# Shift and scale of a streaming-encoder layer: raw fp32 weights over four column groups in place of split weights over 8 columns

## Chip, cores and metric

The kernel runs on one NeuronCore of one Trainium2 chip. The metric is the device time in microseconds; each kernel is timed in several runs, and the median counts. A profile is one execution recorded by the hardware profiler. PE is the matmul engine (PEld its weight loads), DVE the vector engine, ACT the scalar engine, POOL the general one, SP the engine that issues most DMAs.

## The reference, cut to what matters

One layer works on 256 prompt rows and 32 sample rows of 2048 features. Each group has its own conditioning vector `c`; from it come shift, scale and gate, and the first two make `h`, which everything after multiplies with its weights:

```python
mod = jax.nn.silu(c) @ ada_w + ada_b            # (2 vectors of 2048) @ (2048, 3 * 2048)
shift, scale, gate = jnp.split(mod, 3, axis=-1)
h = rms_norm(x, g_pre) * (1.0 + scale[:, None]) + shift[:, None]
proj = h @ w_in                                  # (288 rows of 2048) @ (2048, 20480)
```

After that come a gated convolution, a retention with eight heads, two branch products and an output product. All data is fp32. Only shift and scale, 2 x 2048 x 2048 weights of `ada_w`, are touched by the change.

## The kernel before, in words

Features lie on the 128 partitions: 2048 features are 16 feature tiles, and `h` is held transposed, 128 features by 288 rows for each tile. A product of fp32 data is made of three faster products of type fp32r: `split` (L114) writes a value as `hi` (a cast on ACT, L116) plus `lo` (a subtraction on DVE, L117), and `accumulate` (L146) adds hi x hi, hi x lo and lo x hi (L151, L152, L154). Weights come from memory in loads of 1 MB (`weights`, L127, issued on SP at L131) into `raw` buffers, four of them and a fifth during the first phase. `split_weights` (L134) cuts a load into two pieces of 128 x 1024 and splits each into a `whi` and a `wlo` buffer; there are six of each in the first phase. A `raw` buffer is free for the next load when both of its pieces are split.

The first phase, which the change is in, makes `h` in four groups of four feature tiles (`GROUPS`) and starts on it at once:

- `norm_x` and `turn_x` normalise `x` and turn it, three PE transposes for each of 16 tiles (L257), copied out by ACT and DVE in turn (L258).
- `modulation` (L261) makes scale and shift of one group, 512 features each. The conditioning vectors are the stationary operand (`cs`, silu of c in hi and lo, and zeros around them, so that a slice of 8 columns holds them at rows 4 to 7 for shift or 0 to 3 for scale), and the split weights move, 512 columns at a time, into 8 rows of one PSUM tile (L273). A group takes eight loads (called steps below), each with four feature tiles of K for scale or for shift: two pieces, four products of `whi` and four of `wlo`. Then the 8 rows are copied out (`modrow`, L278), turned by four PE transposes (L282), and the rows of the parts are summed (L284).
- `make_h` (L288) adds bias and factors (L300 to L302), then per feature tile writes `h` (ACT L311 for the prompt, DVE L308 for the sample) and splits it into `hh` and `hl`.
- `first_products` (L313) multiplies the group with four blocks of 512 columns of `w_in` (`FIRST`), one 1 MB load and 48 matmuls each, and adds them into `firsts` (ACT L329 for the first group, DVE L331 for the rest).

The steps of the next group's modulation are put between the four blocks of the present group (the loop with `STEPS`): block 1, four steps, block 2, four steps, then blocks 3 and 4. The loads stand on SP in that same order. The tile framework then orders each engine's instructions by its own priorities, and every engine runs its list strictly in that order. After the first phase (from about 195 us on) PE runs the big products to the end.

Of the kernel before, what the change touches and what calls it, by code (L numbers as in the profile page):

```python
# [10 lines left out]
F32 = mybir.dt.float32  # L11
F32R = mybir.dt.float32r
AF = mybir.ActivationFunctionType
ALU = mybir.AluOpType
PSUM = bass.MemoryType.PSUM

P = 128
D = 2048
# [9 lines left out]
EPS = 1e-6  # L28
# [5 lines left out]
# in the first phase that many more  # L34
MORE_RAW, MORE_PARTS = 1, 2
PIECE = 1024
# feature tiles whose shift and scale come first, and so on
GROUPS = ((0, 4), (4, 8), (8, 12), (12, 16))
# the steps of each: two products of a part of K at a time, then h
STEPS = [sum(2 * min(4, b - k) + 1 for k in range(a, b, 4)) for a, b in GROUPS]  # L40
# rows of the vector table
R_SC, R_CW, R_CB, R_GP, R_AB = 0, 2, 5, 6, 7
NR = 8
# columns of w_in
# [7 lines left out]
# columns of w_in whose products start before all of h is there (2 WC each): q and k of four heads, v of some  # L52
# [3 lines left out]
# decay table: one head's columns  # L56
# [3 lines left out]
def tables():  # L60
    """Rotary and decay constants of the shapes."""
# [25 lines left out]
    # k's factor, in what multiplies it  # L87
# [6 lines left out]
def hybrid_step(ctx: ExitStack, tc, x_prompt, x_sample, c_prompt, c_sample, state_conv, state_ret,  # L94
# [19 lines left out]
    def split(src, hi, lo):  # L114
        """src as hi + lo exactly, each of 12 significant bits."""
        A.copy(out=hi, in_=src)  # L116
        V.tensor_tensor(out=lo, in0=src, in1=hi.bitcast(F32), op=ALU.subtract)  # L117
# [3 lines left out]
    def buffer(tag, size, dtype, bufs, extra):  # L121
        """One of bufs in turn, and of extra ones while there is room for them"""
# [4 lines left out]
    def weights(w, k0, n, col, width):  # L127
        """Rows of n feature tiles from k0, some columns."""
# [5 lines left out]
    def split_weights(raw):  # L134
        """(first row, hi, lo) of each piece"""
# [10 lines left out]
    def accumulate(ps, hi, lo, f, k0, xh, xl, first, last):  # L146
        """ps += (x @ w).T for one tile of w's columns, by the products of the parts"""
# [10 lines left out]
    def product(w, col, xh, xl):  # L158
        """Two tiles of (x @ w[:, col : col + WC]).T, accumulated in PSUM."""
# [22 lines left out]
    def rstd_of(ss, n, width):  # L182
        """(ss / n + EPS) ** -0.5"""
# [10 lines left out]
    cs = const.tile([P, NK, 12], F32R, name="cs")  # L194
# [7 lines left out]
    with tc.tile_pool(name="start", bufs=1, reuse_waits="tile") as st:  # L202
        more.append(st)
        A.preload_act_table(AF.Sigmoid)
        # vectors as rows of P features; they turn in one step
# [23 lines left out]
        V.memset(cs.bitcast(F32), 0.0)  # L229
        split(sc, cs[:, :, 4:6], cs[:, :, 6:8])  # L230
# [9 lines left out]
        def norm_x():  # L240
            """the norm before, then features on the partitions"""
# [19 lines left out]
        def modulation(ka, n):  # L261
            """scale and shift of n feature tiles, the parts' products on rows of their own"""
            pm = aux_tile()
            width = n * P
            step = KH * WC // width
            for part in range(2):
                rows_at = slice(4 - 4 * part, 12 - 4 * part)
                for k0 in range(0, NK, step):
                    for kb, hi, lo in split_weights(weights(ada_w[0], k0, step, (1 - part) * D + ka * P, width)):
                        for k in range(hi.shape[1]):  # L270
                            kt = k0 + kb + k
                            for w in (hi, lo):
                                nc.tensor.matmul(pm[:8, :width], cs[:, kt, rows_at], w[:, k, :],  # L273
                                                 start=(part == 0 and kt == 0 and w is hi),
                                                 stop=(part == 1 and kt == NK - 1 and w is lo))
                    yield
            ms = st.tile([8, 2 * WC], F32, name="modrow", tag="modrow", bufs=2)
            A.copy(out=ms[:, :width], in_=pm[:8, :width])  # L278
            yield
            po = aux_tile()  # L280
            for f in range(n):
                nc.tensor.transpose(out=po[:, 8 * f:8 * f + 8], in_=ms[:, f * P:(f + 1) * P], identity=ident[:8, :8])  # L282
            mod = st.tile([P, 4, 2, 2], F32, name="mod", tag="mod", bufs=2)
# [427 lines left out]
```

## Time and profile before

| what | value |
|---|---|
| time, median of 3 runs | 1395.62 us (1394.64 to 1400.27) |
| span of the profiled execution | 1394.6 us |
| mean granted PE clock | 0.996 |
| busy over the span: PE, DVE, ACT | 98%, 63%, 44% |
| first of the first products on PE | 47.44 us |
| first products of the four groups begin at | 47.4, 88.2, 129.0, 169.9 us |
| end of the first phase | about 195 us |

The profiled execution's own time is its span, 1394.6 us; the runs' median is 1.0 us above it. Matmul rows overlap, so the distance between two starts says what a matmul costs in a stream, not the length of a row. Rows with "x4" merge four instructions that follow on one another. In a row of a matmul, "128\*8 128x512" means a stationary operand of 128 rows by 8 columns, and a moving one of 128 x 512.

### The profile page before, as it was taken

Reading aid. Unit: us, or ns where it says so; the run is one execution under the profiler, and the core shown is the slowest. Engines: PE = TensorE matmul, PEld = TensorE weight load, DVE = VectorE, ACT = ScalarE, POOL = GpSimd, SP = SyncE. Lnnn points to the kernel's source line nnn. Section 1 sums busy time; section 2 is a strip of 40 time slices with the busy share of each in tenths; the row PEclk is TensorE's granted clock in tenths of the full one; section 3 lists DMA queues with packets and bytes.
Section 4 is the critical chain, followed back from the end, with each engine's and each line's share of the span. In section 5 each row is a group of like instructions: output and inputs, shape, how many; then the busy total and the mean of one; then the engine's idle time right before and its main releaser. Section 6 shows DMA issues by size and latency. Waiting matters only on the chain.

```text
span 1394.6 us, 23833 instructions
## 1 busy us (share of the span) xinstructions
PE 1362.2 (98%) x9978; PEld 1300.2 (93%) x9978; DVE 872.9 (63%) x1426; ACT 612.0 (44%) x885; POOL 9.4 (1%) x16
## 2 busy tenths in 40 slices
PE   4999999999999999999999999999999999999996
PEld 1677898999999999999999999999999999999995
DVE  5888977555545866666777868766555334555443
ACT  6876645544444333333333333333333333334442
POOL 0000000000000000000000000000000000000000
PEclk9999999999999999999999999999999999999998
DMA  9988853444444667566565657574544555556531
GB/s 330 333 305 309 302 173 126 156 152 139 160 160 142 190 210 215 185 207 207 188 206 192 215 183 223 178 247 153 179 154 162 172 160 173 160 173 227 160 104 68
DMA packets 234069, 267.79 MB, mean 192 GB/s; under 512 B 5077, under 2 KB 208133, under 8 KB 233349
## 3 DMA queue, kind: packets, MB, share of 16 engines
q1 hardware_dynamic: 227968, 256.22, 55.6%
q10 hardware_dynamic: 5992, 10.04, 2.5%
q8 instruction: 78, 1.28, 0.4%
q14 instruction: 31, 0.25, 0.0%
HBM read 261.75 MB, written 4.49 MB: 191 GB/s over the span
## 4 chain that ended last, share of the span: by engine, by line
issue 67%; PE 31%; DVE 1%; DMA 0%; ACT 0%; SPq 0%; POOL 0%; DVEq 0%; POOLq 0%; ACTq 0%
PE acc L151 8%; PE acc L152 7%; PE acc L154 7%; PE aux L273 4%; PE aux L390 1%; PE aux L392 1%; PE aux L257 1%; PE aux L391 1%; PE aux L490 0%; DMA x<-in_x_prompt_dram 0%; DVE wlo L117 0%; PE aux L404 0%; DVE x L680 0%; PE aux L440 0%; ACT xT L247 0%
## 5 line engine op out<-in xcount | busy, mean ns | idle before, releaser
L117 DVE TENSOR_TENSOR wlo<-raw,whi 128x1024 fp32r<-128x1024 f32 x448 | 542.0, 1221 | 402.8 <-ACT whi L116 402.3
L116 ACT CAST whi<-raw 128x1024 fp32r<-128x1024 f32 x448 | 464.1, 1049 | 583.4 <-PE acc L152 550.6
L152 PE MATMUL acc<-hl,whi 128*128 128x288 f32 x2304 | 632.4, 296 | 0.0
L151 PE MATMUL acc<-hh,whi 128*128 128x288 f32 x2304 | 631.1, 296 | 0.0
L151 PEld LDWEIGHTS acc<-hh,whi 128*128 128x128 f32 x2304 | 432.4, 188 | 3.2 <-issue 1.1
L152 PEld LDWEIGHTS acc<-hl,whi 128*128 128x128 f32 x2304 | 433.2, 188 | 1.0 <-DVE hl L117 0.3
L154 PE MATMUL acc<-hh,wlo 128*128 128x288 f32 x2304 | 406.2, 293 | 0.0
L154 PEld LDWEIGHTS acc<-hh,wlo 128*128 128x128 f32 x2304 | 341.5, 188 | 0.2 <-issue 0.2
L525 DVE SCALAR_TENSOR_TENSOR gbc<-raw,sc,gbc 128x256 f32<-128x256 f32 x240 | 100.4, 476 | 10.5 <-DMA raw<-in_ada_w_dram 10.5
L152 PE MATMUL acc<-ml,whi 128*128 128x288 f32 x256 | 70.9, 297 | 0.0
L151 PE MATMUL acc<-mh,whi 128*128 128x288 f32 x256 | 70.8, 299 | 0.0
L152 PE MATMUL acc<-yl,whi 128*128 128x288 f32 x256 | 70.0, 295 | 0.0
L151 PE MATMUL acc<-yh,whi 128*128 128x288 f32 x256 | 70.0, 296 | 0.0
L151 PE MATMUL acc<-ch,whi 128*128 128x288 f32 x256 | 70.0, 296 | 0.0
L152 PE MATMUL acc<-cl,whi 128*128 128x288 f32 x256 | 69.5, 294 | 0.0
L273 PE MATMUL aux<-wlo,cs 128*8 128x512 f32 x128 | 51.3, 401 | 0.4
L273 PE MATMUL aux<-whi,cs 128*8 128x512 f32 x128 | 51.6, 403 | 0.0
L151 PEld LDWEIGHTS acc<-mh,whi 128*128 128x128 f32 x256 | 48.3, 189 | 0.1
L152 PEld LDWEIGHTS acc<-cl,whi 128*128 128x128 f32 x256 | 48.3, 189 | 0.0
L152 PEld LDWEIGHTS acc<-yl,whi 128*128 128x128 f32 x256 | 48.2, 188 | 0.1
L152 PEld LDWEIGHTS acc<-ml,whi 128*128 128x128 f32 x256 | 48.1, 188 | 0.1
L151 PEld LDWEIGHTS acc<-yh,whi 128*128 128x128 f32 x256 | 48.1, 188 | 0.1
(188 smaller groups left out, 967.2 us busy)
## 6 DMA issues: line engine op xcount, KB each, us to landing
raw<-in_w_in_dram SPq DMA_DIRECT2D x144, 1024.0 KB, 5.2
raw<-in_ada_w_dram SPq DMA_DIRECT2D x48, 1024.0 KB, 6.2
raw<-in_w_branch_dram SPq DMA_DIRECT2D x32, 1024.0 KB, 5.7
raw<-in_w_out_dram SPq DMA_DIRECT2D x16, 1024.0 KB, 5.7
x<-in_x_prompt_dram SPq DMA_DIRECT2D x2, 1024.0 KB, 6.1
out_dram<-ns SPq DMA_DIRECT2D x16, 128.0 KB, 2.9
x<-in_x_prompt_dram ACTq DMA_DIRECT2D x1, 2048.0 KB, 8.0
out_dram<-x ACTq DMA_DIRECT2D x4, 512.0 KB, 2.8
```

The lines of the kernel that those rows point to most:

```text
L116: A.copy(out=hi, in_=src)
L117: V.tensor_tensor(out=lo, in0=src, in1=hi.bitcast(F32), op=ALU.subtract)
L151: nc.tensor.matmul(ps, hi[:, k, fs], xh[:, k0 + k, :], start=first and k == 0, stop=False)
L152: nc.tensor.matmul(ps, hi[:, k, fs], xl[:, k0 + k, :], start=False, stop=False)
L154: nc.tensor.matmul(ps, lo[:, k, fs], xh[:, k0 + k, :], start=False, stop=last and k == n - 1)
L257: nc.tensor.transpose(out=px[:, g * P:g * P + n], in_=x[:n, g, k * P:(k + 1) * P], identity=ident[:n, :n])
L273: nc.tensor.matmul(pm[:8, :width], cs[:, kt, rows_at], w[:, k, :], start=(part == 0 and kt == 0 and w is hi), stop=(part == 1 and kt == NK ...
L390: nc.tensor.matmul(ps, a[0][ai], b[0][bi], start=first, stop=False)
L391: nc.tensor.matmul(ps, a[0][ai], b[1][bi], start=False, stop=False)
L392: nc.tensor.matmul(ps, a[1][ai], b[0][bi], start=False, stop=last)
L525: V.scalar_tensor_tensor(out=ga[:, b], in0=raw[:, k], scalar=sc[:, kt, b:b + 1], in1=ga[:, b], op0=ALU.mult, op1=ALU.add)
```

## The change

`cs` becomes 32 columns of fp32, silu of both vectors in the first two and zeros behind, not split. A step loads two feature tiles of K for both shift and scale, in two DMAs of 512 KB into one `raw` buffer, and the raw fp32 weights are the moving operand: four products for each step, each with 32 stationary columns, at four positions of the array and of the PSUM tile's partitions (`tile_position`): 0 and 32 for an even feature tile's shift and scale, 64 and 96 for an odd one's. The `raw` buffer is free when the last of the four has run. The 128 rows are copied out, and four fp32 products with `pick` (a 128 x 4 matrix of ones and zeros) turn and sum them; the vector engine reads the result in place, without the sum of L284. Line numbers behind this place in the file are four or five higher after the change: L273 becomes L281, L278 L285, L282 L289, L300 to L302 L305 to L307, L311 L316.

```diff
-    cs = const.tile([P, NK, 12], F32R, name="cs")
+    cs = const.tile([P, NK, 32], F32, name="cs")
+    pick = const.tile([P, 4], F32, name="pick")
+    rows4 = ident.rearrange("p (k s r) -> p k s r", k=2, s=2)
+    V.tensor_tensor(out=pick.rearrange("p (s b) -> p s b", s=2), in0=rows4[:, 0, :, 0:2], in1=rows4[:, 1, :, 0:2], op=ALU.add)
...
-        V.memset(cs.bitcast(F32), 0.0)
-        split(sc, cs[:, :, 4:6], cs[:, :, 6:8])
+        V.memset(cs, 0.0)
+        V.tensor_copy(cs[:, :, 0:2], sc)
...
-            step = KH * WC // width
-            for part in range(2):
-                rows_at = slice(4 - 4 * part, 12 - 4 * part)
-                for k0 in range(0, NK, step):
-                    for kb, hi, lo in split_weights(weights(ada_w[0], k0, step, (1 - part) * D + ka * P, width)):
-                        for k in range(hi.shape[1]):
-                            kt = k0 + kb + k
-                            for w in (hi, lo):
-                                nc.tensor.matmul(pm[:8, :width], cs[:, kt, rows_at], w[:, k, :],
-                                                 start=(part == 0 and kt == 0 and w is hi),
-                                                 stop=(part == 1 and kt == NK - 1 and w is lo))
-                    yield
-            ms = st.tile([8, 2 * WC], F32, name="modrow", tag="modrow", bufs=2)
-            A.copy(out=ms[:, :width], in_=pm[:8, :width])
+            step = KH * WC // (2 * width)
+            for k0 in range(0, NK, step):
+                raw = buffer("raw", KH * WC, F32, RAW, MORE_RAW)
+                v = raw.rearrange("p (k s c) -> p k s c", k=step, s=2)
+                for s in range(2):
+                    c0 = s * D + ka * P
+                    nc.sync.dma_start(out=v[:, :, s, :], in_=ada_w[0, k0 * P:(k0 + step) * P, c0:c0 + width]
+                                      .rearrange("(k p) c -> p k c", p=P))
+                for k in range(step):
+                    kt = k0 + k
+                    for s in range(2):
+                        g = 32 * (2 * (kt % 2) + s)
+                        nc.tensor.matmul(pm[g:g + 32, :width], cs[:, kt, :], v[:, k, s, :], start=kt < 2, stop=kt >= NK - 2,
+                                         tile_position=(0, g))
+                yield
+            ms = st.tile([P, 2 * WC], F32, name="modrow", tag="modrow", bufs=2)
+            A.copy(out=ms[:, :width], in_=pm[:, :width])
             yield
             po = aux_tile()
             for f in range(n):
-                nc.tensor.transpose(out=po[:, 8 * f:8 * f + 8], in_=ms[:, f * P:(f + 1) * P], identity=ident[:8, :8])
-            mod = st.tile([P, 4, 2, 2], F32, name="mod", tag="mod", bufs=2)
-            V.tensor_reduce(out=mod[:, :n], in_=po[:, :8 * n].rearrange("p (f s r b) -> p f s b r", s=2, r=2, b=2),
-                            axis=mybir.AxisListType.X, op=ALU.add)
-            return mod[:, :n, 0, :], mod[:, :n, 1, :]
+                nc.tensor.matmul(po[:, 4 * f:4 * f + 4], ms[:, f * P:(f + 1) * P], pick, start=True, stop=True)
+            mod = po[:, :4 * n].rearrange("p (f s b) -> p f s b", s=2, b=2)
+            return mod[:, :, 1, :], mod[:, :, 0, :]
```

The change also moves instructions. On PE, the place behind block 2 of group 0's first products, where the second four steps of group 1's modulation end (before: `aux_460` is the modulation's PSUM tile, `whi_681` block 3's weights).

```order
L273 MATMUL aux_460<-whi_663,cs_87 8x512
L273 MATMUL aux_460<-wlo_664,cs_87 8x512
L273 MATMUL aux_460<-whi_663,cs_87 8x512
L273 MATMUL aux_460<-wlo_664,cs_87 8x512
L151 MATMUL acc_675<-hh_85,whi_681 128x288
```

The same place on PE after the change, where `aux_371` is that PSUM tile, `raw_466` to `raw_487` are the four steps and `whi_504` is block 3's weights:

```order
L154 MATMUL acc_407<-hh_85,wlo_439 128x288 x2
L281 MATMUL aux_371<-raw_466,cs_87 32x512 x4
L281 MATMUL aux_371<-raw_473,cs_87 32x512 x4
L281 MATMUL aux_371<-raw_480,cs_87 32x512 x4
L281 MATMUL aux_371<-raw_487,cs_87 32x512 x4
L289 MATMUL aux_562<-pick_88,modrow_560 128x4 x4
L151 MATMUL acc_498<-hh_85,whi_504 128x288
```

Before, block 3 follows the last step at once, and the four transposes L282 stand behind block 3; now the four products with `pick` stand between the last step and block 3.

On ACT at the same place before, with the casts of the last step (`raw_653`), of block 3 (`raw_679`) and of block 4 (`raw_777`):

```order
L116 CAST whi_655<-raw_653 128x1024
L116 CAST whi_663<-raw_653 128x1024
L116 CAST whi_681<-raw_679 128x1024
L116 CAST whi_709<-raw_679 128x1024
L278 COPY modrow_737<-aux_460 8x512
L116 CAST whi_779<-raw_777 128x1024
```

And on ACT after, from the copies that end block 2 of group 0:

```order
L334 COPY firsts_94<-acc_407 128x288
L285 COPY modrow_560<-aux_371 128x512
L316 ACTIVATE h_570<-xT_122,add_370,mul_369 128x256
L316 ACTIVATE h_575<-xT_122,add_370,mul_369 128x256
L116 CAST hh_85<-h_570 128x288
L116 CAST hh_85<-h_575 128x288
L116 CAST whi_504<-raw_502 128x1024
```

Before, block 3's weights are cast ahead of the copy of `modrow`; now their cast stands behind that copy and behind the first two tiles of the new `h`. The two other groups that prepare a next one have the same order, before and after.

## The prediction, made blind

> **What bounds the kernel now.** I read the page's head first, then a table of busy times by stage, then the first phase's rows in order of time. The head says that PE is the bound over the span as a whole:
>
> ```profile
> span 1394.6 us, 23833 instructions
> PE 1362.2 (98%) x9978; PEld 1300.2 (93%) x9978; DVE 872.9 (63%) x1426; ACT 612.0 (44%) x885; POOL 9.4 (1%) x16
> ```
>
> The change touches only the first phase, so I cut the span at that phase's marks. The columns are: stretch, its length, then busy us (and instructions) of PE, PEld, DVE, ACT and POOL, the granted PE clock, the DMA engines' busy share, GB/s.
>
> ```profile
> 0.00:17.65 17.65, 0.78 (x2) 0.36 (x2) 2.76 (x12) 9.47 (x11) 1.56 (x7) 1.00 0.82 284
> 17.65:41.67 24.02, 22.30 (x83) 7.72 (x83) 23.26 (x23) 16.99 (x21) 0.00 (x0) 1.00 1.03 374
> 41.67:47.44 5.77, 5.77 (x34) 3.66 (x34) 3.69 (x13) 3.95 (x9) 0.00 (x0) 1.00 1.05 387
> 47.44:88.22 40.78, 40.78 (x261) 31.50 (x261) 34.72 (x45) 34.10 (x53) 0.00 (x0) 1.00 0.92 332
> 88.22:129.00 40.78, 40.78 (x263) 31.61 (x261) 35.26 (x46) 27.59 (x35) 0.00 (x0) 1.00 0.90 320
> 129.00:169.90 40.90, 40.90 (x263) 31.57 (x262) 37.53 (x58) 29.19 (x38) 0.00 (x0) 1.00 0.85 299
> 169.90:195.00 25.10, 25.10 (x193) 25.10 (x192) 16.49 (x26) 8.93 (x11) 0.00 (x0) 1.00 0.57 181
> 195.00:1394.60 1199.60, 1185.80 (x8890) 1168.65 (x8889) 719.20 (x1210) 481.80 (x712) 7.88 (x9) 1.00 0.54 174
> ```
>
> Four things are to be seen. From 195 us on PE is the limit and nothing changes there, so the gain or loss is how much earlier or later the first phase ends. In 47 to 170 us, three groups of 40.8 us, PE never pauses, yet DMA runs at 85 to 92%. The last group, first products alone, takes 25.1 us: 192 matmuls at 0.131 us, 6.27 us for a block. And in 17.65 to 41.67 DVE is 97% busy.
>
> That DVE time is the splits of the first eight steps, which end only at 42 us:
>
> ```profile
> 28.65 13.71 DVE L117 TENSOR_TENSOR wlo<-raw,whi 128x1024 fp32r<-128x1024 f32 x12 [0.76 <-ACT whi L116]
> L117 DVE TENSOR_TENSOR wlo<-raw,whi 128x1024 fp32r<-128x1024 f32 x100 | 116.8, 1218 | 18.2 <-ACT whi L116 18.0
> ```
>
> **The change part by part.** *Removed.* For four groups 8 steps x 2 pieces = 64 splits of weights: 64 x 1.22 = 78 us of DVE and 64 x 1.05 = 67 us of ACT. In the three groups of 40.8 us PE hides them, so they are worth something only in the first stretch. PE's products of a step, 8 x 0.235 us:
>
> ```profile
> 88.22 0.40 PE L273 MATMUL aux<-whi,cs 128*8 128x512 f32 x1
> 88.46 0.40 PE L273 MATMUL aux<-wlo,cs 128*8 128x512 f32 x1
> ...
> 88.93 0.40 PE L273 MATMUL aux<-wlo,cs 128*8 128x512 f32 x1
> 89.17 0.29 PE L151 MATMUL acc<-hh,whi 128*128 128x288 f32 x1
> ```
>
> A group's PE time comes out: 25.1 + 64 x 0.2375 = 15.2 + 0.34 for the transposes = 40.6 of the 40.8 us.
>
> *Added on PE.* The step's four fp32 products. The trace has fp32 products at L440, of 256 columns, each as two records:
>
> ```profile
> 208.88 0.60 PE L440 MATMUL aux<-firsts 128*128 128x256 f32 x2
> 209.32 0.38 PE L441 MATMUL aux<-firsts 128*128 128x128 f32 x2
> 209.63 0.25 PE L442 MATMUL aux<-firsts 128*32 128x32 f32 x2
> 209.81 0.40 PE L151 MATMUL acc<-hh,whi 128*128 128x288 f32 x1
> ```
>
> One takes 0.44 us, so one of 512 columns 0.88. No matmul in this trace shares the array with another, so the price of a step is bounded only: 4 x 0.88 = 3.52 us if the four column groups take turns, 0.88 if all four run at once, against 1.9 now. I take 0.88, because the four use different columns and different output partitions and nothing in the program orders them; 3.52 is a rival. [...]
>
> *Moved: block 3's cast.* Behind the last step of a group PE now finds the products with `pick`, then block 3, whose weights ACT casts only after `modrow` and two tiles of `h`. Before, ACT went from the steps to those casts and PE never waited. The chain has these rows:
>
> ```profile
> 75.27 0.58 ACT L278 COPY modrow<-aux 8x512 f32<-8x512 f32 x1 [2.22 <-PE aux L273]
> 195.90 0.59 ACT L116 CAST vh<-aux 128x512 fp32r<-128x512 f32 x1 [4.08 <-PE aux L404]
> 82.20 0.16 DVE L302 TENSOR_TENSOR add<-mod,vecs 128x8 f32<-128x8 f32 x1
> 83.61 1.10 ACT L311 ACTIVATE h<-xT,add,mul 128x256 f32<-128x256 f32 x2 [0.24 <-DVE mul L301]
> 84.61 0.75 ACT L116 CAST hh<-h 128x288 fp32r<-128x288 f32 x2
> 85.27 1.05 ACT L116 CAST whi<-raw 128x1024 fp32r<-128x1024 f32 x1
> ```
>
> The copy of 128 x 512 costs 0.59 like the cast from PSUM of that size; four `pick` products 4 x 0.18 = 0.72 by L442's two records; three small DVE steps 0.48 (the sum of L284 is gone); then 1.10 + 0.75 + 1.05; with about 0.3 of latencies 5.0 us, in which PE does only the 0.72. Queued behind it on PE are blocks 3 and 4 and the next group's block 1.
>
> *Moved: the release of buffers.* Now DVE's splits free the `raw` buffers, running ahead of PE into six pieces; after the change a step's buffer is free only when PE has come to it. The queue's waits in 47 to 170 us and a load's time from issue to landing:
>
> ```profile
> SPq L131 <- DVE wlo L117: 83.6, 30, 9.3
> raw<-in_w_in_dram SPq DMA_DIRECT2D x144, 1024.0 KB, 5.2
> ```
>
> At 387 GB/s (row 41.67:47.44) loads that follow one another land every 2.7 us. So a group has a loop: at its first step the five buffers hold four steps and block 2. That step (0.88) frees one; the next four steps land after 5.2 + 3 x 2.7 = 13.3; the last takes 0.88, the chain 5.0, blocks 3, 4 and the next block 1 18.8: 38.9 us, 1.9 less than now, although PE's work is only 25.1 + 7.0 + 0.7 = 32.8. SP issues twice as many DMAs for a step, same bytes in rows of the same 2 KB; it has time.
>
> *The start.* The end of the first modulation before:
>
> ```profile
> 40.61 0.39 PE L273 MATMUL aux<-wlo,cs 128*8 128x512 f32 x1
> 41.67 0.41 PE L282 MATMUL aux<-ident,modrow 8*128 8x8 f32 x4 [0.67 <-ACT modrow L278]
> 42.01 5.50 PE L257 MATMUL aux<-ident,x 128*128 128x128 f32 x30
> 47.44 0.79 PE L151 MATMUL acc<-hh,whi 128*128 128x288 f32 x4
> L258 ACT COPY xT<-aux 128x288 f32<-128x288 f32 x8 | 3.1, 397 | 7.1 <-PE aux L257 7.1
> ```
>
> Without splits the last step ends with its load. The phase has then read 2.46 MB of x and vectors and 8 x 1.05 MB: 10.85 MB, of which 17.65 x 284 = 5.01 by 17.65 us and the rest at 374 GB/s, 15.6 us: 33.3. Then 0.88 + 0.2, copy 0.59, `pick` 0.8, DVE 0.5: 36.2. ACT has to do, ahead of block 1's cast, four tiles of `h` (2 x 1.10 + 2 x 0.75), five copies of 0.40 and the cast: 6.75. First product at 43.0 instead of 47.4: 4.4 us gained. The 30 transposes (5.4 us on PE) run beside it.
>
> *Sum, four at once.* Group 0: block 1 frees its buffer at about 45.3, block 2's load lands at 50.5, the next four steps to 61.3; + 0.88 + 5.0 + two blocks 12.5 = 79.7, where before 88.2 stood: 8.5 gained. Two more loops, 2 x 1.9: 12.3. The last group is unchanged. Against that stands the clock. Behind 9 us of idle PE ran these products at 0.43 us each, nearly double:
>
> ```profile
> 22.62 0.63 PE L273 MATMUL aux<-wlo,cs 128*8 128x512 f32 x1
> 23.05 0.63 PE L273 MATMUL aux<-whi,cs 128*8 128x512 f32 x1
> ```
>
> (the granted clock reads 1.00 there all the same). The chain leaves PE idle for 4.3 us in each of three groups, and in the first 34 us PE is sparsely used; if each gap brought that pace back for 2.2 us it would cost 1 us; I put 3 us on all three, bounds 0 and 8 (6 us at that pace each). [...]
>
> 12.3 - 3 = 9 us: the span goes from 1394.6 to about 1385.6, the median from 1395.6 to 1387, since it stands 1.0 above the span. Small edits (`pick`, a wider `cs`) fall where DVE waits for the vectors before 9 us; uncovered they cost under 0.5 us.
>
> **The rivals.** *Two at once.* L440 shows that an fp32 product is two records. If records start strictly in order and the second needs the columns of the first, only the second record of one product and the first of the next overlap: 0.44 per product, 1.76 per step. Then the start gains 3.5, group 0 ends at 86.3 (1.9 gained), and the two loops become PE's own, 25.1 + 14.1 + 5.0 = 44.2, 3.4 more each: 4.7 slower, 1400. [...] For it: the two records. Against: the four products share neither columns nor output partitions.
>
> *In turn (slower).* The four column groups take turns, 3.52 a step. The point from which the change loses is about 1.55 us a step. The start: 17.65 + 28.2 + 1.5 of transposes + 8.7 = 56.0, 8.6 late; group 0 54.7 (+13.9), two of 25.1 + 28.2 + 5.0 = 58.3 (+17.5 each): 57 us slower, 1453. For it: nothing in the trace runs side by side. Against: the different columns.
>
> *No loop.* If neither buffers nor chain bind (ACT's and DVE's new slack, earlier landings), groups cost 33 us, PE and DMA alike (12 x 2.7): 4.4 + 3 x 7.8 = 28 faster, 1368. Against it: the order on ACT and PE, which is fixed.
>
> **How the numbers follow.** Four at once 0.45, two at once 0.28, in turn 0.20, no loop 0.05, between two and one 0.02. The forecast is four at once, 1387; its own bounds are 1383 (no clock loss) to 1392. The range reaches down to 1367, where no loop lies, and up to 1410, which holds two at once with the clock's bound of 8 us on top; left out is in turn. About 0.5%, 7 us, is what a measurement of this kernel tells from no change. Faster by more: 0.32 of four at once, and no loop: 0.37. Within: 0.13 of four at once, 0.18 of two at once: 0.31. Slower: 0.10 of two at once (with clock losses), in turn, the rest: 0.32.
>
> **What would show it.** Right: no casts and splits of `ada_w`; first product near 43 us; a step's four products starting within 0.9 us together; a PE gap of 4 to 5 us behind each group's last step, ended by block 3's cast; groups of about 39 us; the DMA queue waiting for PE instead of DVE. Wrong: step products 0.44 or 0.88 us apart (rivals one, two), no gap behind the last step, or groups near 33 us.

## The result, and the profile after

The changed kernel takes 1409.92 us (median of 4 runs, 1408.83 to 1410.72), the kernel before, on the same chip, 1397.94 us (median of 4 runs, 1394.64 to 1400.86): ratio 1.0094, 95% interval 1.0076 to 1.0111. Two of those four runs took 1400 instead of 1395, like the profiled execution of 1400.25 us whose clock was halved at the start (experiment 3); against the other two the changed kernel loses 14.8 us. The forecast was 1387, about 10 us faster; by the medians the result is 12 us slower. The profiled execution has a span of 1408.5 us, 13.9 more than before:

```profile
span 1408.5 us, 23656 instructions
...
PE 1362.4 (97%) x9994; PEld 1304.9 (93%) x9994; DVE 802.5 (57%) x1359; ACT 551.3 (39%) x820; POOL 9.2 (1%) x16
```

DVE and ACT have lost the 70 and 61 us of splits that the change takes away. PE has the same busy time as before (1362.4 us for 1362.2) although a step's products, queued, take 0.89 us instead of 1.9. The table by stage of the changed kernel says why (stretch, length, busy us and instructions of PE, PEld, DVE, ACT, POOL, granted PE clock, DMA share, GB/s):

```profile
36.12:47.30 11.18, 11.18 (x47) 5.66 (x47) 5.34 (x17) 6.53 (x15) 0.00 (x0) 0.55 0.99 365
47.30:55.39 8.09, 8.09 (x53) 7.93 (x49) 1.97 (x2) 1.73 (x4) 0.00 (x0) 0.78 0.61 220
55.39:95.33 39.94, 35.69 (x257) 29.43 (x256) 13.77 (x22) 18.61 (x32) 0.00 (x0) 0.91 0.83 299
95.33:138.99 43.66, 38.70 (x265) 30.60 (x265) 19.24 (x35) 11.67 (x17) 0.00 (x0) 0.92 0.81 289
138.99:182.60 43.61, 38.89 (x265) 31.16 (x265) 24.22 (x40) 14.86 (x21) 0.00 (x0) 0.92 0.85 300
182.60:201.50 18.90, 18.90 (x147) 18.90 (x146) 11.35 (x25) 7.18 (x12) 0.00 (x0) 1.00 0.58 184
201.50:1408.50 1207.00, 1193.04 (x8890) 1176.09 (x8888) 719.92 (x1204) 481.52 (x710) 7.66 (x9) 1.00 0.54 173
```

From one group's block 1 to the next's it takes 40 to 44 us where about 37 (the first) and 38.9 were forecast (the table before is cut ahead of block 1, this one behind it). The first phase ends at 201.5 (before: 195), 6.5 us late. And the part behind it, which the change does not touch, takes 1207.0 us instead of 1199.6 for the same 8890 matmuls: 7.4 more. So two separate losses of about 7 us are to be explained, and a gain that did not come.

The clock column is the first lead. In the profiled execution of the kernel before it was 1.00 in every stretch. (The profile's clock records begin at 25.5 us there and at 23.6 us here; the 1.00 of a stretch ahead of that says nothing.) A finer cut of the changed kernel, at the start and behind the second group's last step:

```profile
33.00:36.50 3.50, 2.49 (x12) 0.67 (x12) 0.00 (x0) 0.59 (x1) 0.00 (x0) 1.00 1.04 385
36.50:50.70 14.20, 14.20 (x59) 8.68 (x59) 7.31 (x18) 7.06 (x15) 0.00 (x0) 0.53 0.77 282
...
112.00:115.50 3.50, 1.71 (x14) 0.97 (x8) 0.87 (x5) 1.18 (x3) 0.00 (x0) 1.00 1.05 388
115.50:122.50 7.00, 4.85 (x20) 4.86 (x21) 5.57 (x9) 7.00 (x13) 0.00 (x0) 0.52 1.05 387
```

The granted clock is halved for 14 us at the start (37.3 to 50.9 by the clock records) and for about 7 us behind the chain (115.8 to 122.6). PE's rows in order of time at the start show what it does to the work (columns: start, us, engine, line, tiles, count, idle time before and its releaser):

```profile
34.36 1.06 PE L281 MATMUL aux<-raw,cs 128*32 128x512 f32 x6 [0.31 <-DMA raw<-in_ada_w_dram]
36.12 1.05 PE L289 MATMUL aux<-pick,modrow 128*128 128x4 f32 x8 [0.69 <-ACT modrow L285]
37.03 8.47 PE L261 MATMUL aux<-ident,x 128*128 128x128 f32 x30
45.43 1.94 PE L281 MATMUL aux<-raw,cs 128*32 128x512 f32 x8
47.30 0.61 PE L151 MATMUL acc<-hh,whi 128*128 128x288 f32 x1
```

`pick` starts at 36.1, five and a half us earlier than the transposes of the sums did before. But then the 30 transposes take 8.4 us instead of 5.4, the next step 1.9 instead of 0.9, and the first product comes at 47.3, where it came before. Block 1 takes 8.1 instead of 6.3.

Four queued steps, and the chain behind the second group's last step, in PE's rows:

```profile
95.33 3.64 PE L281 MATMUL aux<-raw,cs 128*32 128x512 f32 x32
98.90 0.40 PE L151 MATMUL acc<-hh,whi 128*128 128x288 f32 x1
...
111.60 1.06 PE L281 MATMUL aux<-raw,cs 128*32 128x512 f32 x6 [0.31 <-DMA raw<-in_ada_w_dram]
113.35 1.05 PE L289 MATMUL aux<-pick,modrow 128*128 128x4 f32 x8 [0.69 <-ACT modrow L285]
117.65 0.61 PE L151 MATMUL acc<-hh,whi 128*128 128x288 f32 x1 [3.24 <-ACT whi L116]
```

The same chain in ACT's rows:

```profile
112.71 0.59 ACT L285 COPY modrow<-aux 128x512 f32<-128x512 f32 x1 [20.16 <-PE aux L281]
...
116.56 1.99 ACT L116 CAST whi<-raw 128x1024 fp32r<-128x1024 f32 x2
```

98.90 - 95.33 = 3.57 us for four steps, 0.89 each, where run 6 below has 3.48 in one column group: the four column groups do run at once. The chain takes 117.65 - 112.71 = 4.9 us. Both are what was forecast.

The longest two of the DMA queue's waits up to the end of the phase (us in total, times, longest):

```profile
SPq L131 <- DVE wlo L117: 45.1, 7, 15.6
SPq L275 <- PE aux L281: 42.1, 15, 10.4
```

For the steps' loads (L275) it is mostly PE's steps (L281) that set free the buffers now, no longer the splits on DVE. The loads of `w_in` (L131) still wait longest for splits, their own.

### The profile page after: what moved, and what is told of

Its sections match the earlier page's. It is cut to its first block, busy times and chain, and to the rows that moved or that the text cites. A ratio compares the mean times of both kernels' runs of the same rounds, so it can differ in the third digit from the quotient of the medians.

```text
span 1408.5 us, 23656 instructions
## 1 busy us (share of the span) xinstructions
PE 1362.4 (97%) x9994; PEld 1304.9 (93%) x9994; DVE 802.5 (57%) x1359; ACT 551.3 (39%) x820; POOL 9.2 (1%) x16
## 4 chain that ended last, share of the span: by engine, by line
issue 67%; PE 28%; DMA 3%; ACT 1%; SPq 1%; DVE 1%; POOL 0%; DVEq 0%; POOLq 0%; ACTq 0%
PE acc L151 7%; PE acc L152 7%; PE acc L154 7%; DMA raw<-in_ada_w_dram 3%; PE aux L281 1%; PE aux L261 1%; PE aux L395 1%; PE aux L397 1%; PE aux L396 1%; SPq L275 1%; PE aux L495 0%; DMA x<-in_x_prompt_dram 0%; PE aux L409 0%; PE aux L289 0%; DVE x L685 0%
## 5 line engine op out<-in xcount | busy, mean ns | idle before, releaser
L117 DVE TENSOR_TENSOR wlo<-raw,whi 128x1024 fp32r<-128x1024 f32 x384 | 468.2, 1222 | 406.1 <-ACT whi L116 405.2
L151 PE MATMUL acc<-hh,whi 128*128 128x288 f32 x2304 | 642.4, 300 | 9.7 <-ACT whi L116 9.7
L152 PE MATMUL acc<-hl,whi 128*128 128x288 f32 x2304 | 643.0, 299 | 0.0
L116 ACT CAST whi<-raw 128x1024 fp32r<-128x1024 f32 x384 | 401.8, 1050 | 593.2 <-PE acc L152 543.6
L151 PEld LDWEIGHTS acc<-hh,whi 128*128 128x128 f32 x2304 | 437.2, 190 | 16.2 <-ACT whi L116 12.5
L154 PEld LDWEIGHTS acc<-hh,wlo 128*128 128x128 f32 x2304 | 346.0, 189 | 0.0
L151 PEld LDWEIGHTS acc<-ch,whi 128*128 128x128 f32 x256 | 48.1, 188 | 0.0
L281 PE MATMUL aux<-raw,cs 128*32 128x512 f32 x256 | 42.0, 638 | 3.1 <-DMA raw<-in_ada_w_dram 2.9
```

The source lines that it names most:

```text
L151: nc.tensor.matmul(ps, hi[:, k, fs], xh[:, k0 + k, :], start=first and k == 0, stop=False)
L152: nc.tensor.matmul(ps, hi[:, k, fs], xl[:, k0 + k, :], start=False, stop=False)
L154: nc.tensor.matmul(ps, lo[:, k, fs], xh[:, k0 + k, :], start=False, stop=last and k == n - 1)
L281: nc.tensor.matmul(pm[g:g + 32, :width], cs[:, kt, :], v[:, k, s, :], start=kt < 2, stop=kt >= NK - 2, tile_position=(0, g))
```

## The experiments

The theories at this point: the halved clock (13 us in all, by the rows above), the loop of buffers that only PE sets free, the chain, and, for the 7 us behind the first phase, addresses of tiles or mere chance. Ratios are to the kernel before on the same chip, so that 1.0094 is the changed kernel's. A gain in us, where the text names one, is the difference of two ratios; the differences of the times are 0.7 to 2.2 us larger for runs 1 to 5, since two of the four runs of the kernel before behind the 1.0094 took 1400.

**1. PE kept busy.** Unused products behind steps and chain:

```diff
+WARM = 14
...
+                if ka == 0 or k0 >= NK // 2:
+                    for k in range(step):
+                        nc.tensor.matmul(idle[:, :P], ident, v[:, k, 1, :P], start=True, stop=True)
...
+            for f in range(WARM if ka else 0):
+                nc.tensor.matmul(idle[:, :P], ident, ms[:, f % n * P:(f % n + 1) * P], start=True, stop=True)
```

> The changed kernel with extra fp32 products of 128 columns into a scratch tile: two behind each step of the first group's modulation and of steps 5 to 8 of the others, and 14 (3.1 us of PE) behind the pick products of groups 2 to 4; their results are not used. Theory 'clock': the halved granted clock is what the prediction mis-sized, 3.0 us on the 30 transposes, 1.0 on the next step, 1.8 on block 1 at the start, and 2.6 us behind each of the three chains. Then the granted clock stays at 1.00, the transposes take 5.5 us instead of 8.5, a loop is about 41 us instead of 43.7, and the time falls by 8 to 13 us from 1410 to about 1399. Rival 'loads': what PE wins it waits for the loads instead, the loop stays at 43 to 44 and the time at 1407 to 1411.

1404.87 us, ratio 1.0069 (1.0053 to 1.0085), so 3.5 us less than the changed kernel. Its table by stage:

```profile
26.00:40.00 14.00, 13.94 (x91) 6.32 (x90) 0.91 (x2) 1.39 (x3) 0.00 (x0) 1.00 0.94 328
40.00:54.00 14.00, 14.00 (x66) 9.30 (x66) 7.32 (x18) 6.96 (x15) 0.00 (x0) 0.63 0.82 283
54.00:198.00 144.00, 143.77 (x1088) 121.54 (x1087) 67.60 (x120) 52.95 (x82) 0.00 (x0) 1.00 0.83 296
```

The three dips behind the chains are gone. The loop, from one batch of four steps to the next, is 138.41 - 97.23 = 41.2 instead of 43.7 us (starts of two such rows of 32 on PE).

At the start the dip only moved to 43 us, although PE was busy for 9.74 of the 9.80 us ahead of it, and the unused products themselves delayed `pick` from 36.1 to 39.8. The theory holds for the chains and misses at the start.

**2. The same behind the chain alone.** Only the second of these two edits:

> The changed kernel with 14 products of 128 columns into a scratch tile (results not used) behind the pick products of groups 2 to 4 alone, none in the steps and none at the start. Theory 'clock': PE stays busy in the chain, the granted clock stays at 1.00 from 52 us on, blocks behind a chain run at full pace, and each of three loops is 2.6 us shorter: time about 1402, first phase's end at 193 to 195. Rival 'the loads take it back': block 1 ends earlier but the next steps wait for their loads, end at 199 to 202, time 1407 to 1411.

1403.09 us, ratio 1.0061 (1.0047 to 1.0075): near the expected 1402 and below the 1407 to 1411 of the rival, though by the ratios the gain is 4.6 us where 8 were expected. In the profiled execution, the slowest of its six (1407.47), one of the three chains' dips is gone and two remain, one of them behind a late load. The second group, PE's rows:

```profile
113.08 3.37 PE L291 MATMUL aux<-modrow,ident 128*128 128x128 f32 x28
116.47 0.40 PE L151 MATMUL acc<-hh,whi 128*128 128x288 f32 x1
```

Block 3 starts at full pace, and the loop is 135.70 - 95.47 = 40.2 where no dip fell in it; the next, with a dip (153 to 161 us), takes 44.3 (to the phase's end at 198.8, less 18.8 for the last three blocks).

**3. The start kept busy.** One unused product behind steps 5 to 8 of the first group and one for each of the ten tiles of `x` turned later:

```diff
+            if k >= 6:
+                nc.tensor.matmul(idle[0][:, :P], ident, x[:, 0, k * P:(k + 1) * P], start=True, stop=True)
...
+                if ka == 0 and k0 >= NK // 2:
+                    nc.tensor.matmul(idle[0][:, :P], ident, v[:, 1, 1, :P], start=True, stop=True)
```

> The changed kernel with one fp32 product of 128 columns into a scratch tile behind each of steps 5 to 8 of the first group's modulation, and one for each of the ten tiles of x that are turned behind them (results not used; 14 products, about 3.5 us of PE). Theory 'the sparse stretch at the start halves the clock': with PE busy there the granted clock stays at 1.00 to block 1, the transposes take 5.5 us and the ten products up to 2.5 beside them, block 1 takes 6.3 us instead of 8.1, its end comes at 51 to 53 instead of 55.4, and the time falls by 2 to 5 us to 1405 to 1408. Rival 'transposes count as idle for the clock': the dip comes all the same, only later, as when the steps alone were filled up; block 1 ends at 56 to 59, time 1410 to 1413.

1404.71 us, ratio 1.0062 (1.0044 to 1.0080). The stretch from 36 us to the end of block 1, and PE's rows:

```profile
36.00:53.31 17.31, 17.29 (x122) 13.56 (x116) 7.31 (x18) 8.74 (x19) 0.00 (x0) 1.00 0.83 301
```

```profile
45.70 1.06 PE L283 MATMUL aux<-raw,cs 128*32 128x512 f32 x8
46.79 0.40 PE L151 MATMUL acc<-hh,whi 128*128 128x288 f32 x1
```

No dip, the lone step takes 1.06 instead of 1.94, block 1 ends at 53.3 instead of 55.4 though 14 products were added, and the phase at 197.35 instead of 201.5. The four runs (1404.29 to 1405.88) bear it out, 4.5 us under the changed kernel by the ratios. So the dip at the start goes with the stretch of late steps, `pick` and transposes: with 14 products put into it the profile shows none. That the steps are sparse isn't needed for it: in run 1 (dip at 43.3 us), and in run 6 below (at 54.3), it came with PE at least 99% busy in the 10 us before, the last 3.5 and 5.3 of them with `pick` and transposes alone. Nor is the dip new. In the kernel before with 128 unused bytes (experiment 7), in a profiled execution of 1400.25 us, it lies at 43.5 to 53.7 us, and the same 30 transposes take 7.7 us instead of 5.4:

```profile
41.67:47.44 5.77, 5.68 (x26) 3.44 (x27) 2.98 (x11) 3.83 (x9) 0.00 (x0) 0.66 1.04 391
42.10 7.79 PE L259 MATMUL aux<-ident,x 128*128 128x128 f32 x30
```

Of the 84 runs of the kernel before that were timed beside the experiments 13 took 1399 to 1401 us at a mean clock of 0.993, as this one did, the others 1394 to 1397 at 0.996 or more. The changed kernel had a mean of 0.985 to 0.987 in all four runs, which goes with the four dips of its profile. So, by those clocks, the change made frequent a dip that came in about one run of six before. Filling up the transposes alone wasn't tried, so which part of the stretch brings the dip is not shown.

**4. One more `raw` buffer.** `MORE_RAW, MORE_PARTS = 2, 1` in place of 1, 2:

> The changed kernel with six raw buffers in the first phase instead of five, and five instead of six of whi and wlo each (the same memory). Theory 'buffer loop': one more load is under way when PE is in blocks 1 and 2, so the last step of a group lands 2.7 us earlier, loop 41 instead of 43.7, time 1402 to 1406. Rival 'the chain and the clock set it': loop 43 to 44, time 1408 to 1411.

1399.93 us, ratio 1.0031 (1.0019 to 1.0042): 8.8 us gained, a little more than expected. The loop is 130.62 - 89.64 = 41.0, 2.7 less, as the buffer theory says. In the profiled execution, the fastest of the eleven (1398.14), no dip came at the start; by their mean clocks (0.989 to 0.990, the others 0.985 to 0.987) only three of the eleven were spared it, so the median's gain doesn't come from there:

```profile
36.20 5.56 PE L261 MATMUL aux<-ident,x 128*128 128x128 f32 x30
41.77 1.06 PE L281 MATMUL aux<-raw,cs 128*32 128x512 f32 x8
43.49 0.40 PE L151 MATMUL acc<-hh,whi 128*128 128x288 f32 x1 [0.66 <-ACT whi L116]
```

The first product at 43.49: the forecast's sum for the start (43.0) was about right, for a PE at full clock (with this buffer `pick` starts 0.8 us earlier than in the changed kernel).

**5. Steps spread.** In the loop that places the steps, `done * (own - 1.5)` becomes `done * (own - 0.5)`: 3, 3, 2 steps behind blocks 1, 2, 3, and the chain beside block 4.

> The changed kernel with the steps put 3, 3, 2 behind blocks 1, 2, 3 and the chain (row copy, pick, h) beside block 4, in place of 4, 4 and the chain ahead of block 3. Theory 'chain and buffer loop': a group is long because PE waits for the chain (4.3 us), for four loads in a row that its own steps set free (about 7 us) and then runs at half clock (2.6 us). With shorter batches and a block to cover the chain the loop falls from 43.7 to 33 to 37 us, the limits being the loads (12 x 2.7 = 32.5) and PE (32.8), and the time to 1385 to 1393. Rival 'buffers alone': five buffers that PE sets free keep PE and DMA in turn whatever the order, the loop stays at 40 to 42 and the time at 1400 to 1406.

1395.07 us, ratio 0.9999 (0.9988 to 1.0010): 13 us gained, the whole loss made up. The stretch 60 to 180 us of the changed kernel, and of this one:

```profile
60.00:180.00 120.00, 106.06 (x728) 86.02 (x727) 52.78 (x91) 42.32 (x66) 0.00 (x0) 0.91 0.83 299
```

```profile
60.00:180.00 120.00, 112.71 (x841) 94.98 (x840) 61.89 (x106) 48.19 (x73) 0.00 (x0) 0.99 0.93 329
```

PE is busy 112.7 of 120 us instead of 106.1, at a clock of 0.99 instead of 0.91, and DMA moves 329 GB/s instead of 299. The phase ends at 186.45, so a group takes (186.45 - 46.93 - 25.1) / 3 = 38.1 us: more than the 33 to 37 expected, but well under 43.7. Its end is later than 1385 to 1393 because the 7 us behind the phase are still in it.

**6. The products in turn.** All four products of a pair in one column group:

```diff
-                        nc.tensor.matmul(pm[g:g + 32, :width], cs[:, kt, :], v[:, k, s, :], start=kt < 2, stop=kt >= NK - 2,
-                                         tile_position=(0, g))
+                        nc.tensor.matmul(pm[:32, :width], cs[:, kt, :], v[:, k, s, :], start=kt == 0 and s == 0, stop=kt == NK - 1 and s == 1,
+                                         tile_position=(0, 0))
...
-            A.copy(out=ms[:, :width], in_=pm[:, :width])
+            V.memset(ms, 0.0)
+            A.copy(out=ms[:32, :width], in_=pm[:32, :width])
```

This sums scale and shift into one another, so the kernel leaves out their separation and serves for its time alone.

> The changed kernel with all four products of a pair of feature tiles in the same column group and into the same 32 rows, so that they cannot share the array. What is computed changes: scale and shift are summed into one another, and only those 32 rows are copied out. Theory 'four at once': a step costs 3.5 us instead of 0.89, a batch of four 14 instead of 3.6, a loop about 58 to 60 instead of 43.7, and the time rises by 45 to 60 us to 1455 to 1470. Rival 'the order of the products is worth little, a lone step was slow anyway': under 1425.

1458.54 us, ratio 1.045 (1.0429 to 1.0471). PE's rows of the first product and of a batch of four steps:

```profile
56.00 0.85 PE L151 MATMUL acc<-hh,whi 128*128 128x288 f32 x2
...
68.38 13.92 PE L281 MATMUL aux<-raw,cs 128*32 128x512 f32 x32
```

13.92 / 4 = 3.48 us a step against 0.89: the column groups are worth a factor of 3.9 and about 49 us. The forecast's rival *in turn* had said 56.0 for the first product and 1453 for the time.

**7. The 7 us behind the first phase.** First the kernel before, with 1296 unused bytes behind `cs`, so that all later tiles lie where they lie after the change:

```diff
+    pad = const.tile([P, 324], F32, name="pad")
+    V.memset(pad[:, :1], 0.0)
```

> The kernel before with 1296 bytes more per partition of unused constants (and one memset of one column), so that all tiles behind them lie at the addresses they have in the changed kernel. Theory 'addresses': the 7 us that the changed kernel loses between 690 and 1060 us, where neither its instructions nor its clock differ, come from where the tiles lie; then this runs 5 to 8 us longer than before, about 1404, with matmuls 0.138 us apart in that stretch. Rival 'timing or chance of an execution': 1396 to 1400, matmuls 0.133 us apart.

1403.18 us, ratio 1.0056 (1.0042 to 1.0070): the kernel before, with nothing else changed but one small memset, is 8 us slower. Then the changed kernel with `cs` and `pick` in the first phase's pool and 768 bytes in their place, so that later tiles lie as before:

> The changed kernel with cs and pick in the pool of the first phase, which is gone after it, and 768 unused bytes where cs was, so that every tile that outlives the first phase lies where it lay before the change. Theory 'addresses': the part behind the first phase takes 1199 to 1200 us instead of 1207, the first phase still ends at about 201, time 1400 to 1404. Rival 'something else of the change': 1407 to 1411.

1400.56 us, ratio 1.0036 (1.0024 to 1.0048): the loss behind the phase is gone, 1198.1 us with the phase still ending at 201.5:

```profile
201.54:1399.60 1198.06, 1184.21 (x8890) 1167.33 (x8888) 719.32 (x1204) 480.99 (x710) 7.64 (x9) 1.00 0.55 174
```

What distance costs? The changed kernel with `pick` in 64 bytes instead of 16 (later tiles 1344 bytes higher than before):

> The changed kernel with the tile pick widened from 16 to 64 bytes per partition (its first four columns are used), so that all tiles behind cs and pick lie 1344 = 21 x 64 bytes above their place in the kernel before instead of 1296. Theory 'alignment to 64': the 7 us behind the first phase come from the 16 odd bytes; then the part behind the first phase takes 1199.5 us as before instead of 1207, and the time is about 1402. Rival 'another distance or larger unit': it stays at 1206 to 1207, time 1407 to 1411.

1408.23 us, ratio 1.0090 (1.0076 to 1.0104): nothing gained. The kernel before with pads of other sizes, by the first diff of this part:

> The kernel before with 512 unused bytes per partition behind cs, so that all later tiles lie 512 bytes higher. Theory 'a large unit': only the distance from some coarse boundary matters, and 512 bytes cost part of the 7 to 8 us that 1296 bytes cost. Rival 'a unit of 512 or less decides': as before, 1394 to 1397, since 1296 and 1344 are no multiples of 128 and 512 is.

> The kernel before with 1024 unused bytes per partition behind cs. Theory 'a large unit': 1400 to 1404, like 1296. Rival 'a unit of 1024 or less decides': as before, 1394 to 1397.

> The kernel before with 128 unused bytes per partition behind cs. 512 and 1024 bytes changed nothing, 1296 and 1344 cost 7 to 8 us. Theory 'any offset that is no multiple of 512 costs': 1400 to 1404. Rival 'only what is no multiple of 128 costs': 1394 to 1397.

> The kernel before with 256 unused bytes per partition behind cs. Theory 'any offset that is no multiple of 512 costs': 1400 to 1404. Rival 'a unit of 256 or 128 decides': 1394 to 1397.

> The kernel before with 64 unused bytes per partition behind cs. 128, 256, 512 and 1024 bytes changed nothing, 1296 and 1344 cost 7 to 8 us. Theory 'offsets that are no multiple of 128 cost': 1400 to 1404. Rival 'a distance above 1024 costs': 1394 to 1397.

> The kernel before with 1280 = 10 x 128 unused bytes per partition behind cs, what the wider cs alone moves the tiles by. Theory 'offsets that are no multiple of 128 cost': 1394 to 1397. Rival 'a distance above 1024 costs': 1400 to 1404.

| pad behind `cs`, bytes | 64 | 128 | 256 | 512 | 1024 | 1280 | 1296 |
|---|---|---|---|---|---|---|---|
| us | 1405.58 | 1396.39 | 1395.76 | 1395.62 | 1395.70 | 1394.58 | 1403.18 |
| ratio to before | 1.0082 | 1.0005 | 0.9996 | 0.9996 | 0.9997 | 0.9994 | 1.0056 |
| us behind the first phase, profiled execution | 1206.3 | 1199.4 | 1199.0 | 1198.9 | 1199.3 | 1198.1 | 1206.6 |

Multiples of 128, up to 1280, cost nothing that these times tell (with 128 itself the stretch below holds 2261 matmuls, so a third of the loss may be there); 64 and 1296 cost about 7 us behind the first phase, where the kernel before takes 1199.6. So it isn't the wider `cs` (1280 bytes) that costs, but the 16 bytes of `pick`, which push every later tile off a multiple of 128 from where it was. The changed kernel with `pick` at 128 bytes, the direct test of that, wasn't run. The place is mainly the stage of the short convolution: against the version in place the changed kernel loses nothing up to 708 us, 7.5 us by 1079 us, where that stage has ended, 1.3 in the 100 us behind it, and nothing after. Its stretch 700 to 1000 us in the kernel before, in the changed kernel, with 64 bytes, and with 1280:

```profile
700.00:1000.00 300.00, 300.00 (x2273) 299.58 (x2273) 213.95 (x412) 113.38 (x134) 0.00 (x0) 1.00 0.61 197
```

```profile
700.00:1000.00 300.00, 300.00 (x2236) 299.56 (x2236) 209.46 (x395) 112.14 (x133) 0.00 (x0) 1.00 0.60 194
```

```profile
700.00:1000.00 300.00, 300.00 (x2235) 299.56 (x2234) 211.42 (x408) 111.92 (x131) 0.00 (x0) 1.00 0.60 194
```

```profile
700.00:1000.00 300.00, 300.00 (x2273) 299.57 (x2272) 213.84 (x411) 112.93 (x132) 0.00 (x0) 1.00 0.61 197
```

PE reads 100% busy in all four at clock 1.00; only the count of matmuls tells, 2273 or 2235, 0.1320 or 0.1342 us each, 1.7%. The 400 us from 250 to 650, with the same products, hold 2961 before and 2960 after. Which of the later tiles suffers from its address there, and in what way, wasn't tried.

**8. Together.** Spread steps, six `raw` buffers, and `cs` and `pick` in the first phase's pool:

> The changed kernel with three edits together: steps 3, 3, 2 behind blocks 1, 2, 3 with the chain beside block 4; six raw buffers and five of whi and wlo; cs and pick in the first phase's pool, so that later tiles lie where they lay before the change. Theory 'the three costs add': the first phase ends at 180 to 186 us (195.1 before, 201.5 after the change), the rest takes 1199.5, the time is 1380 to 1388, 8 to 14 us under the kernel before. Rival 'spread and buffers give the same gain, and the addresses do not matter': 1390 to 1397.

1380.17 us, ratio 0.9896 (0.9881 to 0.9910), faster than both kernels; the phase ends at 179.4. One dip was left, 36 to 51 us. Two attempts on it. All transposes of `x` ahead of the first modulation:

```diff
-        for k in range(2):
+        for k in range(NK):
             turn_x(k)
...
-        for k in range(2, 6):
-            turn_x(k)
         for _ in h0:
             pass
-        for k in range(6, NK):
-            turn_x(k)
```

> The combined version (steps 3, 3, 2; six raw buffers; addresses of before) with the transposes of all 16 tiles of x written ahead of the first modulation instead of ten of them behind it, so that PE does them beside the first steps. Theory 'start': at the start PE and ACT have the rest of the transposes and their copies on the path, and the clock halves over them (36 to 51 us); without them the first product comes at 40 to 43 us instead of 46.5 and the time falls by 3 to 7 us from 1380 to 1373 to 1377. Rival 'the halved clock comes all the same': PE is idle between the steps instead, block 1 runs at half clock, 1378 to 1382.

1383.95 us, ratio 0.9917 (0.9902 to 0.9931): a miss. PE's rows:

```profile
20.05 10.39 PE L263 MATMUL aux<-ident,x 128*128 128x128 f32 x36 [0.28 <-ACT xT L264]
30.36 8.89 PE L283 MATMUL aux<-raw,cs 128*32 128x512 f32 x56
...
43.17 1.05 PE L291 MATMUL aux<-pick,modrow 128*128 128x4 f32 x8 [0.69 <-ACT modrow L287]
```

The transposes stand ahead of the steps on PE, which frees no `raw` buffer until 30 us; `pick` starts at 43.2 instead of 35.4 in the combined version. That is the loop of buffers again. Then the unused products of run 3:

> The combined version (steps 3, 3, 2; six raw buffers; addresses of before) with the same 14 unused products at the start. Theory 'the sparse stretch halves the clock': block 1 ends 2 to 4 us earlier and the time is 1376 to 1379 instead of 1380.2. Rival: the dip comes all the same and the products only cost, 1380 to 1384.

1377.08 us, ratio 0.9861 (0.9842 to 0.9879). The clock is 1.00 to the end of the phase, and the phase ends at 175.8:

```profile
45.00:175.80 130.80, 127.67 (x977) 109.33 (x977) 70.59 (x123) 54.94 (x85) 0.00 (x0) 1.00 0.93 330
```

## Why the prediction was wrong

By its own steps, in the spans of the profiled executions (1385.6 forecast, 1408.5 measured, 22.9 apart: about 10 us of clock, 7.4 of addresses, and 5.5 left, of which the loads of two loops explain about 4):

- *Four at once*: right, 0.89 a step for 0.88; against 3.48 in one column group (run 6) the four give 3.48 / 0.89 = 3.9 times. The rivals *two at once* and *in turn* fell with it; the price put on *in turn* was within 6 us (1453 for 1458.5), which is in part luck, since the 7 us of addresses that are in the measured time weren't in the price. *No loop* fell with groups of 40 to 44 us.
- *Chain*: right, 4.9 us for 5.0, ended by block 3's cast. What was sized too small is its consequence, the clock.
- *The start*: the sum of the work was about right (47.3 measured, of which the halved clock made 4.0; 43.49 in the execution of run 4 that kept its clock).
- *Clock loss* is the step that failed first. It was put at 3 us, with bounds 0 to 8, for three gaps. Measured: 4.0 us at the start (3.0 on the transposes, 1.0 on the step), 1.8 in block 1, and 2.4 behind each of three chains (117.65 to 122.5 us at half pace), 13 us in all. The start was not in the term at all: PE was "sparsely used" there in the text, but only the chains' idle time was priced. And a chain was priced at 1 us because the prediction let the half pace last 2.2 us, an assumption; the records of the clock show it for 6.8. Its remark that the granted clock "reads 1.00 there all the same" at 22 us reads a stretch ahead of the first clock record (25.5 us). At the start the clock fell at 37.3 us, where the gaps on PE since 30 us were 0.3 to 0.7 us. Run 1 shows the cause for the chains: with PE filled up all three dips go, and the clock reads 1.00 from 54 to 198 us. In the profile of run 2, with the chains alone filled up, one of the three went. For the start run 3 shows that the dip goes when products are put among the late steps and the transposes; which of the two brings it stays open.
- *Buffer loop*: right in kind, 38.9 for 43.7. Of the 4.8 us, 2.4 are the clock. About 2 are the four next loads: 13.3 us forecast from the first step's end, 111.6 - 96.2 = 15.4 measured. The 5.2 us that the sum took for the first load was the median of the loads of `w_in` over the whole execution. In 47 to 170 us of the kernel before a step's load took 6.9 us, 1.7 more; in the changed kernel its halves took 8.0 over all four groups, and 7.0 in that stretch (the first line is the kernel before in that stretch, the second the changed kernel over the whole execution):

```profile
raw<-in_ada_w_dram SPq DMA_DIRECT2D x20, 1024.0 KB, 6.9
raw<-in_ada_w_dram SPq DMA_DIRECT2D x64, 512.0 KB, 8.0
```

- *Small edits* is the other step that failed. `pick` and a wider `cs` were priced by the time of making them, under 0.5 us. The 16 bytes cost 7.4 us behind the first phase (1207.0 for 1199.6), by where later tiles lie. Without it the loss is 0.36% (run 7, in place; interval 0.24 to 0.48%), less than the 0.5% that the prediction took as the least to be told from no change; with it 0.94%.

The measured 1410 stands at the very end of the stated range, 1367 to 1410. That end had been made for *two at once*, which didn't hold; that the time falls inside is luck.

With both failed steps mended the kernel would probably have been faster: with the addresses of before it takes 1400.6, and the 13 us of clock would take that to about 1388, near the forecast. That last sum is argued: runs 2 and 3, which filled up the chains and the start, gained 9 us together by the ratios, and the runs that come nearest to the sum (8) also spread the steps.

## What to carry to other kernels

When work is taken off PE in a stretch, look at the granted clock of the next 15 us: here it was halved behind a stretch that was 71% busy (2.49 of 3.50 us), and in run 1 behind one that was 99% busy (9.74 of 9.80) and ended in transposes, and the dense work behind it pays (block 1 took 8.1 us instead of 6.3). Look at it in more than one execution, since the dip at the start came in some and not in others. When buffers change from being freed by splits on DVE, ahead of PE, to being freed by PE's own products, shorten the batches between the blocks and cover the dependent chain with one, which here gave back 13 us. And an edit that allocates a tile ahead of others moves them all: compare with a pad of the same size in the old kernel before the new instructions are blamed, and try a size that is a multiple of 128 bytes: in this kernel pads of 128 to 1280 took 1394.58 to 1396.39 us, those of 64 and 1296 took 1405.58 and 1403.18.

## What the runs showed of the hardware

- Four fp32 products of 512 columns in four column groups took 0.89 us together, and 3.48 in one column group (run 6).
- Dips of the granted clock to 0.50 in the first phase lasted 13.6 us and three times 6.8 in the changed kernel, 10.2 in runs 1 and 6, 10.2 and 3.4 in run 5, three times 6.8 in run 4.
- In the changed kernel the granted clock went to 0.50 for 6.8 us behind a chain with idle gaps of 0.7 and 3.2 us, and for 13.6 us behind a stretch in which PE was 71% busy (2.49 of 3.50 us) with gaps of 0.3 to 0.7. In run 1 it did so for 10.2 us behind 9.80 us in which PE was busy for 9.74, with `pick` and transposes last. With one buffer more (run 4) the profiled execution had no dip at the start, and by their mean clocks (0.989 to 0.990, the others 0.985 to 0.987) three of the eleven had none.
- Tiles moved by 64, 1296 or 1344 bytes made the matmuls of one stage 1.7% slower (2235 or 2236 in 300 us for 2273; 2234 with 1296), at an unchanged clock and with PE at 100%; with 1280 bytes there were 2273 again, and with 256, 512 and 1024 the part behind the first phase took 1198.9 to 1199.3 us (before: 1199.6); with 128 bytes (2261) it was at most a third of that, and the part behind the first phase took 1199.4.
